# A three-branch decoder trunk in split fp32: convolution taps held from KI on, shorter steps for two pairs of stick heads, and one gate's turned copies tied to the newest weight parts

## The chip, the cores and the metric

The kernel runs on one core of one Trainium2 chip. The metric is the device time of one execution in microseconds; the time before is 2037.99 us, the median of 3 runs (2033.85 to 2039.13).

## What is computed

Two layers, each of which reads one normalised input of 256 tokens by 2048 channels, projects it with one matrix of 18064 columns, and feeds three token mixers, whose gated results are projected, merged and added to the input. Two of the mixers matter here:

```python
def stick_breaking_attention(q, k, v):          # branch C, 8 heads of 128
    z = einsum('bthd,bshd->bhts', q, k) * dh ** -0.5
    log_beta = log_sigmoid(z)
    log_keep = where(strict, log_sigmoid(-z), 0.0)
    after = cumsum(log_keep, axis=3, reverse=True) - log_keep
    a = where(strict, exp(log_beta + after), 0.0)
    return einsum('bhts,bshd->bthd', a, v)

y = lax.conv_general_dilated(y, conv_w, ...)     # branch B: causal depthwise convolution, 31 taps
y_c = (stick_breaking_attention(qc, kc, vc) * silu(zc)) @ w_c_out
```

Branch A scores keys with an indexer of 16 heads (its queries are QI below), keeps 64 keys for each query, and attends to those.

## The kernel before

**The weight stream.** Every matrix is read in units of 512 KB (128 partitions by 1024 elements; 544 elements in one stage). ScalarE (ACT) casts a unit to its high part `wh` (L265), VectorE (DVE) subtracts to get the low part `wl` (L270), and TensorE (PE) runs the unit's matmuls with both (all on L281). There are three buffers each for `wh` and `wl`, so the cast of a unit waits for PE to be done with the unit three before it.

**Background work.** Everything else is written as generators that are advanced from `background()` after a unit's matmuls: a `yield n` lets n units pass. `turns` come first, then the first two entries of `stages`; `finish()` runs all stages to their end at once. A scheduler then orders each engine's instructions ahead of time, so each engine works through a fixed list, and an instruction that waits holds up all behind it on its engine.

**Stick heads.** `stick(h0)` does two heads: scores on PE (L725, L728), then on ACT absolute value, table load, exponential and logarithm (L731 to L735), on DVE two combinations and the mask (L736 to L741), a split in parts `ph` and `pl` (L394, L395); after a pace of 10 units the prefix sums on PE (L747 to L752), then L753 on DVE, the exponential L754 on ACT, the mask L756 on DVE; after 5 more units the product with the values (L761, L763) and its copy L765 on ACT. The text numbers the pairs of heads 1 to 4. Pairs 1 and 2 run first, 3 and 4 after them.

**The stages around them**, in the order of PE: QA (queries of branch A, turned by a DMA transpose), KI (two units), VA with WI (eight units of 544 elements), KA (four units), then `finish()`, then QI (32 units in eight chunks), then the indexer beside the units of the merge gates, then branch A's attention, the gate of branch C (ZC) and of B (ZB).

**Taps.** Each of the 31 taps of the convolution, for each half of the channels, is four scalings on ACT (L439) and one addition on DVE (L442). They wait in a list; `low()`, which makes `wl`, releases one tap for each unit unless `hold[0]` is set. The last three of all are 228, 227 and 226 columns wide (4x228 and so on in the order).

**Turned copies.** `turn_in` sends a block through a DMA transpose and copies it back as 16-bit halves: one half on DVE (L187), the other on ACT (L189). With `bound` the copies may not stand ahead of the newest `wl` (DVE) and `wh` (ACT); without it the scheduler is free. `gate()` follows the copies with the SiLU (L417), the product (L418) and the split (L394, L395).

Of the kernel before, what the change touches and what calls it, by code (L numbers as in the profile page):

```python
# [34 lines left out]
TURN = (8, 8)  # L35
EARLY = (4, 6)
LATE = (6, 6)
MERGED = ((3, 7), (3, 6), (3, 5))
FAST = ((0, 0), (0, 1))
SCALE = float(128 ** -0.5)  # L40
# [5 lines left out]
O_QC, O_KC, O_VC, O_ZC, O_G = 7824, 8848, 9872, 10896, 11920  # L46
# [8 lines left out]
def trunk(ctx: ExitStack, tc: tile.TileContext, x, xt, w_in, w_a, w_b, w_c, w_out,  # L55
# [38 lines left out]
    def nm(s):  # L94
        uid[0] += 1
        return f"{s}_{uid[0]}"
# [29 lines left out]
    def acc_tile():  # L126
        return ap.tile([P, 2, 512], F32, tag="acc", name=nm("acc"))

    def t4(dt=F32):
        return tp.tile([P, 1024], dt, tag="t4", bufs=8, name=nm("t4"))  # L130
# [36 lines left out]
    def turn_in(src, dst, then=None, slots=True, turn=TURN, early=False):  # L167
        own, cols = words(slots)
        rows = own.rearrange("p (t w d) -> p t w d", t=NT, w=2)
        s16 = src.bitcast(U16).rearrange("p t (d w) -> p t d w", w=2)  # L170
        with tc.high_priority():
            for i in range(2):
                nc.scalar.copy(rows[:, :, i, :], s16[:, :, :, i])

        def steps():
            yield turn[0]
            with tc.high_priority() if turn in MERGED else nullcontext():
                for t in range(NT):
                    nc.sync.dma_start(cols.rearrange("p (g t) -> p g t", g=8)[:, :, t * P:(t + 1) * P],
                                      own[:, t * 1024:(t + 1) * 1024], transpose=True)  # L180
            yield turn[1]
            halves_ = cols.rearrange("p (w f t) -> p w f t", w=2, f=4)
            into = own.bitcast(F32).rearrange("p (f t) -> p f t", f=4) if dst is None else dst
            d16 = into.bitcast(U16).rearrange("p f (t w) -> p f t w", w=2)
            bound = turn == LATE or turn in MERGED
            with tc.issue_after(lows[0].ins) if bound else nullcontext(), tc.high_priority() if bound else nullcontext():
                nc.vector.tensor_copy(d16[:, :, :, 1], halves_[:, 1])  # L187
            with tc.issue_after(highs[0].ins) if bound else nullcontext(), tc.high_priority() if bound else nullcontext():
                (nc.vector.tensor_copy if early else nc.scalar.copy)(d16[:, :, :, 0], halves_[:, 0])  # L189
            if dst is None:  # L190
                then(into, cols.bitcast(F32).rearrange("p (f t) -> p f t", f=4))
            elif then is not None:
                then()

        turns.append([steps(), count[0] + 0])
        advance(turns[-1])

    def start(gen):
        stages.append([gen, 0])

    def finish():
        while stages:
            advance(stages[0])

    hold = [False]
# [145 lines left out]
    def chunk_W(w, c0, act):  # L351
        acc = acc_tile()
        for k0 in range(0, KD, 2):
            background(token_products([acc[:, t, :] for t in range(NT)], 512, unit(w, k0, 2, [(c0, 512)]), act, k0, 2, KD,
                                      range(NT)))
        return acc
# [58 lines left out]
    def gate(c0, o, b, w, hx, park=None, slots=True, turn=TURN):  # L415
        def gated(k, z, v):
            nc.scalar.activation(v, z, AF.Silu)  # L417
            nc.vector.tensor_mul(z, v, o[:, k:k + 4, :])  # L418
            b.extend(parts(4))
            split_at(b, k, 4, z)  # L420
            if park is not None:
                for i in range(k, k + 4, 2):
                    nc.gpsimd.dma_start(park[:, i:i + 2], part(b, slice(0, 2), i, 2))

        for k in range(0, KC, 4):
            turn_in(chunk_W(w, c0 + k * P, hx), None, partial(gated, k), slots, turn)
# [45 lines left out]
    parked = [dp.tile([P, KC, 2, S], F32R, name=f"parked{b}") for b in range(3)]  # L472
# [14 lines left out]
    for layer in range(DEPTH):  # L487
        w = w_in[layer]
        nw = cst[:, C_NW + layer * KD:C_NW + (layer + 1) * KD]
        pr = cst[:, C_PR + layer * P_END:C_PR + (layer + 1) * P_END]  # L490
        hx = parts(KD)
# [212 lines left out]
        qcT = slot()  # L704
# [3 lines left out]
        kcT, vc = slot(), slot()  # L708
        for h in range(0, NH, 4):
            turn_in(chunk_W(w, O_KC + h * P, hx), kcT[:, h:h + 4, :], early=True)  # L710
        vcr = vc.rearrange("p a b -> p (a b)").rearrange("p (t f) -> p t f", t=NT)
# [7 lines left out]
            return (b[:, :512].rearrange("p (h t) -> p h t", h=2)[:, :, 0:P],  # L719
                    b[:, 512:768].rearrange("p (h t) -> p h t", h=2))  # L720

        def stick(h0, qcT=qcT, kcT=kcT, vcr=vcr, diag=diag):
            ps = mm_tile()
            for q in range(2):
                nc.tensor.matmul(ps[:, q * S:(q + 1) * S], kcT[:, h0 + q, 0:P], qcT[:, h0 + q, :],  # L725
                                 start=True, stop=True)
            for q in range(2):
                nc.tensor.matmul(ps[:, 512 + q * P:512 + (q + 1) * P], kcT[:, h0 + q, P:S],  # L728
                                 qcT[:, h0 + q, P:S], start=True, stop=True)
            nk, lb = t4(), t4()  # L730
            ab = nc.scalar.activation(nk[:, :768], ps[:, :768], AF.Abs)  # L731
            with tc.issue_after(ab.ins):
                nc.scalar.preload_act_table_set("natural_log_exp_and_others")
            nc.scalar.activation(nk[:, :768], nk[:, :768], AF.Exp, scale=-1.0)
            nc.scalar.activation(nk[:, :768], nk[:, :768], AF.Ln, bias=1.0)  # L735
            nc.vector.scalar_tensor_tensor(lb[:, :768], ps[:, :768], 0.0, nk[:, :768],  # L736
                                           op0=ALU.min, op1=ALU.subtract)
            nc.vector.scalar_tensor_tensor(nk[:, :768], ps[:, :768], 0.0, nk[:, :768],
                                           op0=ALU.max, op1=ALU.add)
            for d in diag(nk):  # L740
                nc.vector.tensor_mul(d, d, smask2)  # L741
            pr_ = pair(768)
            split(*pr_, nk[:, :768])
            yield 10
            pc = mm_tile()
            for i, v in enumerate(pr_):
                nc.tensor.matmul(pc[:, :512], upper_r, v[:, :512], start=i == 0, stop=False)  # L747
            for i, v in enumerate(pr_):
                nc.tensor.matmul(pc[:, :512].rearrange("p (h t) -> p h t", h=2)[:, :, P:S], ones_r,
                                 v[:, 512:768].rearrange("p (h t) -> p h t", h=2), start=False, stop=i == 1)  # L750
            for i, v in enumerate(pr_):
                nc.tensor.matmul(pc[:, 512:768], upper_r, v[:, 512:768], start=i == 0, stop=i == 1)  # L752
            nc.vector.tensor_sub(lb[:, :768], lb[:, :768], pc[:, :768])  # L753
            nc.scalar.activation(lb[:, :768], lb[:, :768], AF.Exp)  # L754
            for d in diag(lb):
                nc.vector.tensor_mul(d, d, smask2)  # L756
            yield 5
            po = mm_tile()
            for q in range(2):
                vs_ = slice((h0 + q) * P, (h0 + q + 1) * P)  # L760
                nc.tensor.matmul(po[:, q * S:(q + 1) * S], vcr[:, 0, vs_], lb[:, q * S:(q + 1) * S],  # L761
                                 start=True, stop=False)
                nc.tensor.matmul(po[:, q * S + P:(q + 1) * S], vcr[:, 1, vs_],  # L763
                                 lb[:, 512 + q * P:512 + (q + 1) * P], start=False, stop=True)
            nc.scalar.copy(qcT[:, h0:h0 + 2, :], po[:, :512].rearrange("p (h t) -> p h t", h=2))  # L765

        settle()
        for h0 in range(0, NH, 2):
            start(stick(h0))

        qaT = slot()
        def spin(q4):
# [8 lines left out]

        for h in range(0, NH, 4):
            turn_in(chunk_W(w, O_QA + h * P, hx), qaT[:, h:h + 4, :], partial(spin, qaT[:, h:h + 4, :]))
        kaT = t4()[:, :2 * S].rearrange("p (c t) -> p c t", c=2)
        ki = tp.tile([P, 2 * S], F32R, tag="ki", bufs=1, name=nm("ki")).rearrange("p (i c t) -> p i c t", i=2, c=1)
        rope(chunk_T(w, O_KI, P, hx, KD), None, partial(split, ki[:, 0], ki[:, 1]))
# [11 lines left out]
        nc.scalar.copy(wp_[64:128], wf[64:128, :, 1])  # L798
        rope(chunk_T(w, O_KA, 256, hx, KD), kaT)

        hold[0] = True
        finish()
        qa2 = slot(F32R).rearrange("p a b -> p (a b)").rearrange("p (i h t) -> p i h t", i=2, h=NIH)
        qb2 = [slot(F32R).rearrange("p a b -> p (a b)").rearrange("p (h t) -> p h t", h=NIH) for _ in range(2)]
# [194 lines left out]

        for j in range(2, 4):  # L1000
            early(1, j)
        gate(O_ZC, qcT, [], w, hx, parked[2])
        gb = []
        gate(O_ZB, cv, gb, w, hx, slots=False, turn=LATE)
        finish()
# [21 lines left out]
        start(mixtures())  # L1027
        gate(O_ZA, qaT, [], w, hx, parked[0], slots=False, turn=LATE)
        finish()
# [28 lines left out]
        def combine(gate_of=None):  # L1058
            gx = gb
            for n, b in enumerate((1, 2, 0)):  # L1060
# [4 lines left out]
                for j in range(4):  # L1065
# [20 lines left out]
                    if n == 2 and j < 3:  # L1086
                        mx[j], = parts(4)
                        turn_in(mg[j // 2][:, j % 2], None, partial(turned, j), False, MERGED[j])
                    elif n == 2:
# [118 lines left out]
        def emit_x(xc, accs, q, c0, ts):  # L1208
# [10 lines left out]
            else:  # L1219
                x_squares([xc[:, t, :] for t in ts], ssq, q, ts)  # L1220
                if q < 3:
                    turn_in(xc, None, lambda z, v: x_parts(z, xn, c0 // P, nwn, 4), False, MERGED[2])

# [88 lines left out]
```

## Time and profile before

| | |
|---|---|
| median of 3 runs | 2037.99 us (2033.85 to 2039.13) |
| the profiled execution | 2035.96 us, span 2034.1 us |
| PE busy | 2008.7 us, 99% of the span |
| VectorE, ScalarE, GpSimd busy | 1562.2 us (77%), 1401.9 us (69%), 97.1 us (5%) |
| HBM | 213 GB/s over the span |
| mean granted clock of TensorE | 0.997 |

Times of views are microseconds from the start of the span. A row of the timeline gives start, duration, engine, line, operation, out<-in, shapes and how many; in square brackets stands how long the engine had been idle and what ended that. Rows that follow each other on ACT and DVE overlap by about 0.1 us in print, so that a run of them takes about 0.1 us less for each than the printed durations. The two layers run the same program of work; in the stages here, rows of layer 1 stand about 1008 us behind those of layer 0.

### The profile page before, as it was taken

The page shows a single profiled execution, that of the slowest core. Times are in us where ns is not written, and L with a number is a line of the kernel's source. Part 1 is how long each engine was busy: PE and PEld are TensorE (multiplying, and loading weights), DVE is VectorE, ACT ScalarE, POOL GpSimd, SP SyncE. Part 2 cuts the span into 40 slices and gives each one's busy share as a digit, 9 for nine tenths or more (in the row PEclk, how much of TensorE's full clock was granted, in tenths as well). Part 3 has the DMA queues.
Part 4 walks back from the last instruction along what each step waited for, and adds up shares of the span by engine and source line. Part 5 has one row for each costly group of instructions (what it writes and reads, how often), then busy time and mean ns, then how long its engine had stood idle before and what let it go on. Part 6 is the DMA issues. An engine that isn't in the chain of part 4 may idle for free. (4 is left out here: it accounts for less than half of the span.)

```text
span 2034.1 us, 26740 instructions
## 1 busy us (share of the span) xinstructions
PE 2008.7 (99%) x9566; PEld 1700.3 (84%) x9566; DVE 1562.2 (77%) x1708; ACT 1401.9 (69%) x1968; POOL 97.1 (5%) x156
## 2 busy tenths in 40 slices
PE   9999998999999999999999999999999999999998
PEld 7888888988788888888888888889888888888887
DVE  8688888787578888866676888878866788788665
ACT  7899796648766555556658987965588665556653
POOL 0000000000001100110000000000000012002100
PEclk9999999999999999999999999999999999999999
DMA  8787675766888877889967776656678898778983
GB/s 279 216 226 214 181 167 173 222 195 191 234 244 264 269 247 232 263 270 264 258 201 211 218 216 187 168 176 206 189 206 235 241 266 285 224 240 264 270 283 126
DMA packets 340278, 458.60 MB, mean 225 GB/s; under 512 B 109104, under 2 KB 159024, under 8 KB 340016
## 3 DMA queue, kind: packets, MB, share of 16 engines
q1 hardware_dynamic: 327040, 420.82, 70.9%
q0 software_dynamic: 11648, 33.56, 5.0%
q10 hardware_dynamic: 1456, 2.51, 0.4%
q8 instruction: 75, 1.23, 0.2%
q14 instruction: 59, 0.48, 0.1%
HBM read 413.30 MB, written 20.97 MB: 213 GB/s over the span
## 5 line engine op out<-in xcount | busy, mean ns | idle before, releaser
L281 PE MATMUL acc<-wh,s 128*128 128x512 f32 (+2 forms) x4736 | 1155.4, 386 | 2.2 <-ACT wh L265 2.0
L270 DVE TENSOR_TENSOR wl<-raw,wh 128x1024 fp32r<-128x1024 f32 (+1 forms) x714 | 858.2, 1208 | 319.2 <-ACT wh L265 313.5
L281 PEld LDWEIGHTS acc<-wh,s 128*128 128x128 f32 x4736 | 875.7, 188 | 179.6 <-ACT wh L265 3.9
L265 ACT CAST wh<-raw 128x1024 fp32r<-128x1024 f32 (+1 forms) x713 | 738.7, 1039 | 390.0 <-PE acc L281 317.9
L281 PE MATMUL acc<-wl,s 128*128 128x512 f32 (+2 forms) x2368 | 622.7, 385 | 0.8 <-DVE wl L270 0.8
L281 PEld LDWEIGHTS acc<-wl,s 128*128 128x128 f32 x2368 | 439.5, 188 | 90.3 <-DVE wl L270 1.3
L439 ACT ACTIVATE t<-s,cst 128x255 f32<-128x255 f32 (+14 forms) x480 | 199.0, 487 | 0.0
L442 DVE TENSOR_TENSOR s<-s,t 128x1020 f32<-128x1020 f32 (+14 forms) x120 | 138.6, 1155 | 1.5 <-ACT t L439 1.1
L281 PE MATMUL acc<-s,wh 128*128 128x384 f32 (+1 forms) x608 | 125.6, 348 | 0.0
L281 PE MATMUL mm<-wh,s 128*128 128x512 f32 x448 | 119.7, 389 | 0.0
L281 PEld LDWEIGHTS acc<-s,wh 128*128 128x128 f32 x608 | 104.2, 189 | 3.1
L281 PEld LDWEIGHTS mm<-wh,s 128*128 128x128 f32 x448 | 84.1, 188 | 17.4
L265 ACT CAST wh<-s 128x1024 fp32r<-128x1024 f32 x32 | 33.6, 1050 | 68.4 <-DVE s L1106 53.3
L281 PEld LDWEIGHTS acc<-s,wl 128*128 128x128 f32 x608 | 79.6, 191 | 0.9
L281 PE MATMUL acc<-s,wl 128*128 128x192 f32 (+1 forms) x608 | 80.1, 273 | 0.0
L232 POOL COPY sm<-sm 128x3 f32<-128x3 f32 x64 | 47.1, 735 | 564.6 <-ACT sm L231 564.6
L281 PE MATMUL mm<-wl,s 128*128 128x512 f32 x224 | 69.1, 390 | 0.0
L265 ACT CAST wh<-t 128x1024 fp32r<-128x1024 f32 x32 | 33.6, 1050 | 37.7 <-DVE t L1106 27.4
L270 DVE TENSOR_TENSOR wl<-s,wh 128x1024 fp32r<-128x1024 f32 x32 | 39.2, 1225 | 26.3 <-ACT wh L265 26.1
L902 POOL DMA_DIRECT2D gates<-t x8 | 6.0, 744 | 1115.5 <-ACT t L901 1066.3
L281 PEld LDWEIGHTS mm<-wl,s 128*128 128x128 f32 x224 | 41.9, 188 | 9.0 <-DVE wl L270 0.4
L270 DVE TENSOR_TENSOR wl<-t,wh 128x1024 fp32r<-128x1024 f32 x32 | 39.1, 1222 | 9.9 <-ACT wh L265 7.1
(241 smaller groups left out, 1286.3 us busy)
## 6 DMA issues: line engine op xcount, KB each, us to landing
raw<-in_w_in_dram SPq DMA_DIRECT2D x570, 512.0 KB, 4.3
raw<-in_w_out_dram SPq DMA_DIRECT2D x64, 512.0 KB, 5.1
raw<-in_w_b_dram SPq DMA_DIRECT2D x32, 512.0 KB, 5.3
raw<-in_w_c_dram SPq DMA_DIRECT2D x32, 512.0 KB, 5.1
raw<-in_w_a_dram SPq DMA_DIRECT2D x32, 512.0 KB, 5.6
parked<-s POOLq DMA_DIRECT2D x16, 512.0 KB, 5.5
t<-gates POOLq DMA_DIRECT2D x16, 512.0 KB, 6.6
s<-parked POOLq DMA_DIRECT2D x32, 256.0 KB, 5.7
```

The source lines that it names most:

```text
L232: seen = nc.gpsimd.tensor_copy(copy[:, :3], mark)
L265: highs[0] = nc.scalar.copy(u[1], u[0])
L270: sub = nc.vector.tensor_sub(u[2], u[0], u[1].bitcast(F32))
L281: newest[0] = nc.tensor.matmul(o, lhsT, rhs, start=start, stop=stop, skip_group_check=True)
L439: nc.scalar.activation(o[:, i, :S - d], yT[:, c, :S - d], AF.Copy, scale=wq)
L442: nc.vector.tensor_add(to, to, o[:, :, :S - d])
L902: nc.gpsimd.dma_start(gates[b][:, :, j * 512:(j + 1) * 512].rearrange("t p d -> p t d"), sg_)
```

## The change

Three edits.

1. `hold[0] = True` moves from ahead of `finish()` to ahead of KI, so no tap is released during KI, VA and KA either. The last three taps of each layer are released after QI.
2. The pace of pairs 3 and 4 becomes 7 and 4 units; pairs 1 and 2 keep 10 and 5.
3. ZC's gate gets a pair of steps of its own, (8, 9) for (8, 8), and its copies are `bound`.

```diff
+OWN = (8, 9)
+STICK = ((10, 5), (7, 4))
...
-            bound = turn == LATE or turn in MERGED
+            bound = turn in (LATE, OWN) or turn in MERGED
...
-        def stick(h0, qcT=qcT, kcT=kcT, vcr=vcr, diag=diag):
+        def stick(h0, pace, qcT=qcT, kcT=kcT, vcr=vcr, diag=diag):
...
-            yield 10
+            yield pace[0]
...
-            yield 5
+            yield pace[1]
...
-            start(stick(h0))
+            start(stick(h0, STICK[h0 // 4]))
...
             turn_in(chunk_W(w, O_QA + h * P, hx), qaT[:, h:h + 4, :], partial(spin, qaT[:, h:h + 4, :]))
+        hold[0] = True
         kaT = t4()[:, :2 * S].rearrange("p (c t) -> p c t", c=2)
...
         rope(chunk_T(w, O_KA, 256, hx, KD), kaT)
-        hold[0] = True
         finish()
...
-        gate(O_ZC, qcT, [], w, hx, parked[2])
+        gate(O_ZC, qcT, [], w, hx, parked[2], turn=OWN)
```

The order of the SP and POOL queues is the same before and after; PE's differs only where the stick heads stand. In rows of the changed kernel, line numbers are 2 higher than in the profile (3 higher from KI to the end of KA). Names: `s_80` is the convolution's input, `s_336` the queries of QA, `s_137` the queries and then the output of the stick heads, `t_439` and `t_436` pair 3's weights, `t_447` and `t_444` pair 4's.

**ACT, from the taps in KI on.** Before:

```order
L439 ACTIVATE t_409_2417<-s_80_536,cst 128x230 x2
L439 ACTIVATE t_413_2441<-s_80_536,cst 128x229 x4
L439 ACTIVATE t_421_2473<-s_80_536,cst 128x228 x4
L265 CAST wh_2632<-raw_2631 128x544
L765 COPY s_137_854<-mm_2495 128x512
L306 COPY ev_2535<-acc_2466 128x256
L439 ACTIVATE t_426_2507<-s_80_536,cst 128x227 x3
L406 COPY ev_2538<-ev_2535 64x256
```

The same place after:

```order
L441 ACTIVATE t_409_2417<-s_80_536,cst 128x230 x2
L441 ACTIVATE t_413_2441<-s_80_536,cst 128x229 x4
L767 COPY s_137_854<-mm_2489 128x512
L191 COPY s_336_2021<-s_379_2247 128x1024
L267 CAST wh_2614<-raw_2613 128x544
L191 COPY s_336_2021<-s_414_2461 128x1024
L308 COPY ev_2523<-acc_2466 128x256
L767 COPY s_137_854<-mm_2517 128x512
L408 COPY ev_2526<-ev_2523 64x256
```

The taps of 228 columns and less are gone from here, and the two turned copies of QA, which stood among VA's and KA's casts, have moved in.

**DVE, where the last stick heads end**, between KA and QI. Before:

```order
L411 TENSOR_TENSOR t_415_2464<-t_415_2464,ev_2884 128x512
L780 TENSOR_TENSOR s_336_2021<-s_336_2021,ev_2715 128x512
L753 TENSOR_TENSOR t_439_2580<-t_439_2580,mm_2837 128x768
L753 TENSOR_TENSOR t_447_2618<-t_447_2618,mm_2870 128x768
L270 TENSOR_TENSOR wl_3014<-raw_3012,wh_3013 128x1024
L756 TENSOR_TENSOR t_439_2580<-t_439_2580,cst 128x2x128
L756 TENSOR_TENSOR t_439_2580<-t_439_2580,cst 128x256
L756 TENSOR_TENSOR t_447_2618<-t_447_2618,cst 128x2x128
```

After (pair 3's L755 stands 15 rows further up):

```order
L397 TENSOR_TENSOR pl_2610<-t_443_2599,ph_2609 128x768
L782 TENSOR_TENSOR s_336_2021<-s_336_2021,ev_2697 128x512
L758 TENSOR_TENSOR t_436_2562<-t_436_2562,cst 128x2x128
L758 TENSOR_TENSOR t_436_2562<-t_436_2562,cst 128x256
L272 TENSOR_TENSOR wl_2935<-raw_2933,wh_2934 128x1024
L309 TENSOR_TENSOR ev_2869<-acc_2763,ev_2869 128x512
L755 TENSOR_TENSOR t_444_2600<-t_444_2600,mm_2786 128x768
L411 TENSOR_TENSOR t_415_2464<-ev_2869,cst 128x512
L412 TENSOR_TENSOR ev_2872<-ev_2872,cst 128x512
L413 TENSOR_TENSOR t_415_2464<-t_415_2464,ev_2872 128x512
L758 TENSOR_TENSOR t_444_2600<-t_444_2600,cst 128x2x128
```

Pairs 3 and 4 no longer end together: pair 3's mask stands ahead of the rotation of KA (L309 to L413), pair 4's behind it.

On ACT the same place reads, after:

```order
L267 CAST wh_2934<-raw_2933 128x1024
L308 COPY ev_2869<-acc_2763 128x512
L767 COPY s_137_854<-mm_2863 128x512
L408 COPY ev_2872<-ev_2869 64x512
L409 COPY ev_2872<-ev_2869 64x512
L267 CAST wh_2970<-raw_2969 128x1024
L756 ACTIVATE t_444_2600<-t_444_2600 128x768
```

Pair 3's output copy (L767) stands ahead of pair 4's exponential (L756); before, both exponentials stood ahead of both output copies. On PE pair 3's product with the values now stands ahead of QI's first unit and pair 4's behind that unit; before, both stood inside QI's third unit.

**ACT, at ZC's gate.** Before:

```order
L394 CAST ph_4989<-t_814_4801 128x1024
L189 COPY s_835_4927<-s_835_4927 128x1024
L265 CAST wh_5030<-raw_5029 128x1024
L417 ACT_TABLE_LOAD
L417 ACTIVATE s_835_4927<-s_835_4927 128x1024
```

After:

```order
L267 CAST wh_5263<-raw_5262 128x1024
L191 COPY s_835_4927<-s_835_4927 128x1024
L267 CAST wh_5290<-raw_5289 128x1024
L419 ACTIVATE s_835_4927<-s_835_4927 128x1024
L267 CAST wh_5314<-raw_5313 128x1024
```

The second half's copy `s_835` now stands behind 12 more units' casts.

## The prediction

> **What bounds the kernel now.** I read the page's busy times first, then PE's waits, then the clock in stretches around the longest wait, then the timeline of that place, engine by engine.
>
> ```profile
> span 2034.1 us, 26740 instructions
> PE 2008.7 (99%) x9566; PEld 1700.3 (84%) x9566; DVE 1562.2 (77%) x1708; ACT 1401.9 (69%) x1968; POOL 97.1 (5%) x156
> ```
>
> PE bounds the whole: it is idle for 25.4 us of 2034.1. Only that idle time, and time in which PE is busy but slow, can be won. PE's waits:
>
> ```profile
> PE mm L761 <- DVE t L756: 9.1, 2, 4.6
> PE acc L281 <- ACT wh L265: 2.0, 3, 1.1
> PE mm L725 <- ACT s L765: 0.8, 2, 0.4
> ```
>
> More than a third of the idle time is one wait in each layer: stick pairs 3 and 4 end in `finish()`, and their product L761 waits 4.6 us for the mask L756. The stretches show what follows (their columns: length; busy PE, PEld, DVE, ACT, POOL; granted clock; DMA share; GB/s):
>
> ```profile
> 320.00:325.00 5.00, 1.13 (x3) 0.98 (x4) 5.00 (x9) 3.81 (x5) 0.00 (x0) 0.86 0.44 112
> 1333.00:1337.00 4.00, 4.00 (x15) 3.46 (x15) 3.24 (x6) 0.58 (x1) 0.00 (x0) 0.50 0.33 111
> 550.00:560.00 10.00, 8.86 (x39) 7.01 (x39) 4.37 (x5) 4.67 (x5) 1.11 (x2) 1.00 1.02 274
> ```
>
> After 4.6 us of idleness the clock is down to 0.50, and PE, though "busy", does half the work. After the idle 1.1 us at ZC (550 to 560) it stays at 1.00. PE's timeline there, with the first row of layer 1's same stretch and its end:
>
> ```profile
> 277.36 0.60 PE L761 MATMUL mm<-t,s 128*128 128x256 f32 x2
> 278.59 2.07 PE L281 MATMUL acc<-s,wh 128*128 128x512 f32 x8
> 282.69 1.24 PE L281 MATMUL acc<-wh,s 128*128 128x272 f32 x8
> ...
> 298.27 1.99 PE L281 MATMUL acc<-s,wh 128*128 128x512 f32 x8
> ...
> 306.63 0.40 PE L747 MATMUL mm<-ph,upper_r 128*128 128x512 f32 x1
> 307.57 2.00 PE L281 MATMUL acc<-s,wh 128*128 128x512 f32 x8
> 312.94 1.57 PE L281 MATMUL acc<-s,wh 128*128 128x384 f32 x8
> 315.22 1.59 PE L281 MATMUL acc<-s,wh 128*128 128x384 f32 x8
> 323.87 1.19 PE L761 MATMUL mm<-t,s 128*128 128x256 f32 x2 [4.57 <-DVE t L756]
> 328.76 1.57 PE L281 MATMUL acc<-s,wh 128*128 128x384 f32 x8
> 1290.45 1.24 PE L281 MATMUL acc<-wh,s 128*128 128x272 f32 x8
> 1337.80 1.58 PE L281 MATMUL acc<-s,wh 128*128 128x384 f32 x8
> ```
>
> From VA's first unit (282.69) to QI's fourth (328.76) PE takes 46.07 us, in layer 1 47.35. The differences of starts give undisturbed lengths: a pair's product 1.23 (277.36 to 278.59), a KA unit 2.79 (298.27 to 306.63 are three), prefix sums 0.94, a QI unit 2.28.
>
> **The shorter steps (edit 2), with the taps out of the way (edit 1).** I follow the new order of ACT and DVE with durations of these rows:
>
> ```profile
> 277.19 3.88 ACT L439 ACTIVATE t<-s,cst 128x230 f32<-128x230 f32 x10
> 285.21 0.40 ACT L406 COPY ev<-ev 64x256 f32<-64x256 f32 x1 [1.73 <-DVE ev L307]
> 290.64 1.28 ACT L733 ACT_TABLE_LOAD   x1
> 291.93 0.65 ACT L265 CAST wh<-raw 128x544 fp32r<-128x544 f32 x1
> ```
>
> ```profile
> L265 ACT CAST wh<-raw 128x1024 fp32r<-128x1024 f32 x11 | 11.4, 1045 | 2.3 <-PE acc L281 2.2
> L189 ACT COPY s<-s 128x1024 uint16<-128x1024 uint16 x2 | 2.7, 1341 | 0.0
> L776 ACT COPY ev<-s 64x512 f32<-64x512 f32 x4 | 2.5, 620 | 0.6 <-DVE t L411 0.5
> L765 ACT COPY s<-mm 128x512 f32<-128x512 f32 x4 | 2.3, 578 | 3.7 <-PE mm L763 3.7
> L394 ACT CAST ph<-t 128x768 fp32r<-128x768 f32 x2 | 1.7, 832 | 0.0
> L270 DVE TENSOR_TENSOR wl<-raw,wh 128x1024 fp32r<-128x1024 f32 x11 | 13.4, 1222 | 2.7 <-ACT wh L265 2.0 <-PE acc L281 0.5
> L778 DVE TENSOR_TENSOR s<-s,cst 128x512 f32<-128x512 f32 x4 | 2.8, 689 | 0.0
> L395 DVE TENSOR_TENSOR pl<-t,ph 128x768 fp32r<-128x768 f32 x2 | 1.9, 954 | 0.1
> L756 DVE TENSOR_TENSOR t<-t,cst 128x256 f32<-128x256 f32 x4 | 1.4, 422 | 0.0
> 282.47 0.76 DVE L187 COPY s<-s 128x1024 uint16<-128x1024 uint16 x1 [1.76 <-DMA s<-s]
> ```
>
> In a run of them each takes about 0.1 us less than printed.
>
> *Pair 3's prefix sums* now stand ahead of KA, not behind its third unit. ACT from 277.19: six tap scalings (2.3) to 279.5; pair 1's output copy, QA's first turned copy and a cast to 281.8; the second turned copy waits for its transpose, which lands at 282.47 (DVE's row), to 283.7; four small copies of KI and pair 2, with the hand-over to DVE that cost 1.73 us of idleness before, to 285.4. Then five casts of 0.54 (2.7), three copies like L776 (1.9), four operations of 768 columns (3.0), two table loads (2.6), KI's part (0.3), KA's first cast (0.95): 296.9; `ph` is there at 297.7. DVE has KA's first `wl` ahead of `pl`: 298.1, then `pl` to 299.0. PE has VA done at about 297.4 (298.27 less the 0.4 us wait of L725, which goes since pair 2's copy L765 now comes before KI's rotation, and half a microsecond of slow restart, an estimate). So PE waits some 1.5 us in two pieces and starts KA at 299.8.
>
> *Pair 4's prefix sums* stand inside KA's fourth unit. PE: 4 x 2.79 + 0.94 from 299.8 is 311.9. DVE is back to back from 299.0: five `wl` (5.7), four operations of 768 columns (3.5), three of 512 (1.8), two parts of VA (0.7), two masks (1.3): 312.0. So pair 3's product meets its mask within 0.1 us and ends at 313.2.
>
> *Pair 4's product* stands one QI unit later, at 315.5. What it needs starts only at 313.2, since ACT is a fixed list: pair 3's output copy (0.5), KA's two rotations (1.3), a cast (0.95), the exponential (0.84), then DVE's mask (0.75), hand-overs 0.1: 317.7. PE waits 2.2 us. This term is the firmest, since all of it hangs on one event. The product, QI's second and third units (1.23 + 4.56) and 0.2 for the restart bring the fourth to 323.7: 5.1 us earlier than 328.76. Layer 1 loses 1.3 more now (47.35 against 46.07) by a longer slow stretch: 6.4. Together **11.5 us**.
>
> The sum assumes that 2.2 us of idleness leave the clock alone. Bounds: nothing, as after 1.1 us, or the whole price after 4.6 us. In layer 0 that price is 1.7 us (323.87 to 328.76 is 4.89; two products, 2.46, and the rest of the QI unit that they interrupt, about 0.7, are 3.2), in layer 1 1.3 more. I take nothing: 2.2 is nearer 1.1. The Trainium skill ("TensorE: Matmul & The Clock Gate", Part 1) says that the clock halves after a whole idle window of about 3.4 us, in windows that run freely; the halving to 0.50 agrees, and by the rule 2.2 us is safe, so the sum stays.
>
> The table loads speak against the shortened path: two of them lie ahead of `ph`. The cast at 291.93 starts 0.01 us behind the load's end, so I charge 1.29. The Trainium skill ("ScalarE: Activation LUTs", What ACT_TABLE_LOAD costs) adds about 1.38 us of draining to each load, 2.66 in all. That is rival D.
>
> **The held taps (edit 1)** leave 1.6 us of ACT for each of three taps and 1.1 us of DVE beside the indexer.
>
> ```profile
> 290.21 1.09 DVE L442 TENSOR_TENSOR s<-s,t 128x904 f32<-128x904 f32 x1
> 431.40 1.21 DVE L270 TENSOR_TENSOR wl<-raw,wh 128x1024 fp32r<-128x1024 f32 x1
> 435.62 1.07 PE L281 MATMUL acc<-wl,s 128*128 128x512 f32 x4
> ```
>
> DVE then runs up to 3.3 us late. The tightest `wl` that I found there ends at 432.61, and PE uses it at 435.62 (the one before it at 432.90), 3.0 us later: hidden, or 0.3 us uncovered in each layer. I charge 0.3 for both; with no cover it would be 6.6.
>
> **ZC's gate (edit 3).** ACT stands still for a transpose, and the casts behind it with it:
>
> ```profile
> 556.04 1.37 ACT L189 COPY s<-s 128x1024 uint16<-128x1024 uint16 x1 [5.30 <-DMA s<-s]
> 575.52 1.05 ACT L265 CAST wh<-raw 128x1024 fp32r<-128x1024 f32 x1 [1.67 <-PE acc L281]
> PE acc L281 <- ACT wh L265: 0.6, 1, 0.6
> ```
>
> Behind 12 more casts the copy finds its data landed. What PE loses to this are its waits for `wh`, 2.0 us in all, less the one in the first 30 us (0.6, the last row); I take **1.4** (bounds 0 and 2.0). The gate's work of 3.3 us moves beside B's gate, where ACT idles 1.67 us in each unit (575.52).
>
> **Sum.** 11.5 + 1.4 - 0.3 = 12.6 us off 2035.96, the profiled execution's own time: 2023.4. The median of the three runs is 2.0 higher, so theirs would be 2025.4; I say 2024.5, between the two, and add the same 1.1 to each rival's sum.
>
> **Rivals.**
>
> A. *All stick waits vanish.* ACT and DVE rows were padded by waits in my walk; were they quicker by 2 us, nothing would wait. Against it: pair 4's chain of 4.5 us behind one QI unit of 2.28. PE's path from VA to QI's fourth unit would be 14.7 for VA (15.58 less the 0.9), 11.2, 1.9, 2.5 and 6.8, in all 37.0: 9.1 and 10.4 less than now, which with the rest is 2016.5.
>
> B. *Pair 4's wait passes the point where the clock halves.* For it: a late `wl` or cast adds to the 2.2. With 3.5 us of waiting in both layers, and prices of 1.7 and 3.0, the gain falls by 7.3 to 5.3: 2032.
>
> C. *Slower:* the wait moves to pair 3's prefix sums ahead of KA. ScalarE's list has no idle place left there. Turned copies now stand ahead of eight casts, so a transpose that lands late holds VA's casts as well. If the second lands 4 us later than 282.47, pair 3's parts come 4 us later, PE idles over 5, and the clock halves: 8 and 4.7 us in both layers are the whole gain. From there on the kernel is slower, 2042 at 289. Against it: SP's order is the same, and the landing is in the trace.
>
> D. *Each table load costs 1.4 us more.* Pair 3 would come 2.8 later in each layer: 2030. The row of 291.93 speaks against it.
>
> **Chances.** Forecast 0.70, A 0.12, B 0.12, C 0.04, D 0.02. 0.3% (6.1 us) is about what a measurement of this kernel can tell from no change. Faster: the forecast but for 0.03, A, D and a little of B, 0.82; within 0.3%: 0.14; slower: 0.04. The range takes in most of A and of B: 2016 to 2032.
>
> **What would show it.** Right: L761's two waits fall from 4.6 to about 2.2 each, a new one of 1 to 1.5 us for `pl` at L747 stands ahead of KA, granted clock 1.00 from VA to QI, the L725 wait gone, no ACT wait for a DMA at ZC, PE idle about 19 us in all. Wrong: a clock under 0.9 near QI (B), no wait at L761 (A), long waits of ACT on `s` in VA (C), or waits for `wl` beside the indexer.

## The result, and the profile after

The changed kernel takes 2025.95 us (median of four runs, 2025.41 to 2026.60), the kernel before 2036.53 in the same comparison: a ratio of 0.9948, with a 95% interval of 0.9931 to 0.9966. It is faster by 10.6 us. The forecast was 2024.5 with a range of 2016 to 2032. The total came out; which of the edits earned it did not, as the experiments show. Of the eleven executions of e1 below, one ran in a slower state (4080.92 us) and counts in no ratio.

The profiled execution took 2025.73 us. The head of its page, and PE's waits (waiter and what it waited for; us in total, times, longest):

```profile
span 2024.0 us, 26716 instructions
PE 2006.2 (99%) x9566; PEld 1698.9 (84%) x9566; DVE 1560.7 (77%) x1708; ACT 1399.7 (69%) x1966; POOL 98.5 (5%) x156
```

```profile
PE mm L763 <- DVE t L758: 4.1, 2, 2.1
PE mm L749 <- DVE pl L397: 1.8, 2, 0.9
PE acc L283 <- ACT wh L267: 1.5, 4, 0.7
```

PE is idle for 17.8 us instead of 25.4. The wait for the masks has fallen from 4.6 to 2.0 us in each layer, and a new one of 0.9 for `pl` stands ahead of KA. The scores' wait for pair 2's copy is gone, and so are two of 0.6 and 0.5 us in each layer for `ph` and `pl` of pair 4's prefix sums. (All names at the matmul, copy and mask lines are two lines further down than before: L761 is L763, L756 is L758.) PE's timeline from the end of VA to QI, in layer 0, and from the product on in layer 1 (rows in between are left out):

```profile
296.26 1.28 PE L283 MATMUL acc<-wh,s 128*128 128x272 f32 x8 [0.18 <-ACT wh L267]
299.34 0.51 PE L749 MATMUL mm<-pl,upper_r 128*128 128x512 f32 x1 [0.90 <-DVE pl L397]
312.36 0.59 PE L763 MATMUL mm<-t,s 128*128 128x256 f32 x2
313.59 1.66 PE L283 MATMUL acc<-s,wh 128*128 128x384 f32 x8
318.15 0.67 PE L763 MATMUL mm<-t,s 128*128 128x256 f32 x2 [2.03 <-DVE t L758]
320.09 2.61 PE L283 MATMUL acc<-s,wh 128*128 128x384 f32 x8
323.41 1.59 PE L283 MATMUL acc<-s,wh 128*128 128x384 f32 x8
325.70 1.59 PE L283 MATMUL acc<-s,wh 128*128 128x384 f32 x8
1321.29 0.67 PE L763 MATMUL mm<-t,s 128*128 128x256 f32 x2 [2.05 <-DVE t L758]
1322.86 2.91 PE L283 MATMUL acc<-s,wh 128*128 128x384 f32 x8
1326.52 1.57 PE L283 MATMUL acc<-s,wh 128*128 128x384 f32 x8
```

Behind the wait of 2.03 us the first half of QI's second unit takes 2.61 us instead of 1.59, and in layer 1 2.91. The same stretches in numbers, with ZC's (columns as before: length; busy PE, PEld, DVE, ACT, POOL; granted clock; DMA share; GB/s):

```profile
318.00:325.00 7.00, 6.85 (x34) 6.65 (x35) 6.36 (x10) 3.68 (x6) 0.00 (x0) 0.76 0.26 77
1320.00:1326.00 6.00, 4.71 (x20) 4.58 (x21) 5.63 (x10) 3.93 (x7) 0.00 (x0) 0.72 0.32 94
550.00:560.00 10.00, 10.00 (x46) 8.24 (x45) 4.34 (x4) 6.19 (x6) 0.00 (x0) 1.00 0.74 232
```

So the clock still falls in QI. Finer windows put it at 0.50 for 3.41 us in each layer (318.80 to 322.21 and 1322.32 to 1325.73); before, it was 3.41 us in layer 0 (from 323.62) and 6.82 us in layer 1 (from 1330.55). At ZC PE is now busy throughout (8.86 of 10 us before).

One measure serves all that follows: the stretch from the start of VA's first unit to the start of QI's fourth. It was 46.07 us in layer 0 and 47.35 in layer 1; it is now 43.05 (282.65 to 325.70) and 43.11. With nothing to wait for the forecast had put it at 37.0.

### The profile page after: what moved, and what is told of

Its sections match the earlier page's. It is cut to its first block, busy times and chain, and to the rows that moved or that the text cites. A ratio compares the mean times of both kernels' runs of the same rounds, so it can differ in the third digit from the quotient of the medians.

```text
span 2024.0 us, 26716 instructions
## 1 busy us (share of the span) xinstructions
PE 2006.2 (99%) x9566; PEld 1698.9 (84%) x9566; DVE 1560.7 (77%) x1708; ACT 1399.7 (69%) x1966; POOL 98.5 (5%) x156
## 3 DMA queue, kind: packets, MB, share of 16 engines
q8 instruction: 75, 1.23, 0.2%
## 5 line engine op out<-in xcount | busy, mean ns | idle before, releaser
L272 DVE TENSOR_TENSOR wl<-t,wh 128x1024 fp32r<-128x1024 f32 x32 | 39.1, 1222 | 10.2 <-ACT wh L267 7.5
```

The source lines that it names most:

```text
L272: sub = nc.vector.tensor_sub(u[2], u[0], u[1].bitcast(F32))
```

## The experiments

The kernels were timed in five comparisons. Each ratio is to the kernel before in the same comparison, whose median lay between 2034.89 and 2036.53 us, so times from different comparisons (the changed kernel; e1 to e4; e5 to e8; e9 to e11; e12) can be off against each other by 1.6 us, the spread of these medians. Stretches and waits are those of the one profiled execution.

| kernel | time, us | ratio to before, 95% | stretch, layers 0 and 1 | longest mask wait |
|---|---|---|---|---|
| before | 2036.53 | 1 | 46.07, 47.35 | 4.6 |
| changed kernel | 2025.95 | 0.9948 [0.9931, 0.9966] | 43.05, 43.11 | 2.1 |
| e1 steps alone | 2038.02 | 1.0006 [0.9997, 1.0015] | 47.10, 48.03 | 4.0 |
| e2 held taps alone | 2023.77 | 0.9938 [0.9925, 0.9952] | 41.09, 41.17 | 1.0 |
| e3 ZC alone | 2033.41 | 0.9988 [0.9980, 0.9997] | 47.26, 46.87 | 4.6 |
| e4 changed, pair 4's chain first | 2019.18 | 0.9917 [0.9902, 0.9932] | 39.10, 39.09 | none |
| e5 held taps and ZC | 2022.67 | 0.9936 [0.9923, 0.9949] | 41.22, 40.96 | 1.0 |
| e6 e4 with one table load fewer | 2025.17 | 0.9952 [0.9939, 0.9965] | 41.38, 42.80 | 0.8 |
| e7, e8 e4 with later masks (one run each) | 2023.01, 2023.59 | | 40.74, 40.43; 41.39, 40.82 | 1.0; 1.5 |
| e9 one tap held | 2033.82 | 0.9990 [0.9981, 0.9998] | 46.21, 46.49 | 5.2 |
| e10 e5, chains of pairs 3 and 4 first | 2020.24 | 0.9924 [0.9911, 0.9936] | 39.82, 39.81 | 0.6 |
| e11 e4 with steps 8 and 4 | 2019.86 | 0.9921 [0.9908, 0.9935] | 39.53, 38.84 | none |
| e12 before, chains of pairs 3 and 4 first | 2026.53 | 0.9959 [0.9945, 0.9972] | 41.34, 42.34 | 0.9 |

### Each edit by itself (e1, e2, e3, e5)

e1 keeps the shorter steps, puts `hold[0] = True` back ahead of `finish()`, and calls ZC's gate as before:

```diff
-        hold[0] = True
         kaT = t4()[:, :2 * S].rearrange("p (c t) -> p c t", c=2)
...
+        hold[0] = True
         finish()
...
-        gate(O_ZC, qcT, [], w, hx, parked[2], turn=OWN)
+        gate(O_ZC, qcT, [], w, hx, parked[2])
```

> The shorter steps alone (the taps stay where they were, the ZC gate as before). Theory (both are needed): three taps, 1.6 us of ACT each, stand in ACT's list between KI and KA, so the masks come up to 4.8 us later than in the changed kernel and PE waits for them again: at most 4 us faster than before, 2033 to 2037. Rival (the steps do it all): the 8 to 9 us of the two stick edits come without the taps' move: 2028.

Measured: 2038.0 us, no gain at all (the interval of the ratio spans 1). PE's waits in e1:

```profile
PE mm L763 <- DVE t L758: 8.0, 2, 4.0
PE mm L749 <- ACT ph L396: 4.9, 4, 1.6
```

In the kernel before, PE waited 2.2 us in all at the prefix sums (L747 there):

```profile
PE mm L747 <- ACT ph L394: 1.2, 2, 0.6
PE mm L747 <- DVE pl L395: 1.0, 2, 0.5
```

The wait for the masks is 4.0 us instead of 4.6, but that for the parts `ph` and `pl` has grown from 2.2 to 4.9 us, since the prefix sums are asked for earlier. The theory's direction holds; even its 4 us were too many.

e2 keeps the held taps alone; `STICK = ((10, 5), (10, 5))`, and ZC's gate as before.

> The held taps alone (the steps stay 10 and 5, the ZC gate as before). Theory (both are needed): pairs 3 and 4 still end together in QI and their masks, though ACT has 4.8 us less ahead of them, are asked for a QI unit or two earlier; the wait at the product L763 stays over 3 us in each layer: at most 4 us faster than before, 2033 to 2037. Rival (the taps were the whole delay): the wait falls under 1 us, the clock stays at 1.00, and the time falls by 8 or more: 2028.

Measured: 2023.8 us. The rival won: the held taps alone give 12.4 us (ratio 0.9938), no less than the whole change's 10.6 (the two intervals overlap). The theory, that both stick edits are needed, falls. PE's rows at the two products in layer 0, and the stretches around them:

```profile
315.01 0.67 PE L763 MATMUL mm<-t,s 128*128 128x256 f32 x2 [1.04 <-DVE t L758]
...
318.48 0.67 PE L763 MATMUL mm<-t,s 128*128 128x256 f32 x2 [0.94 <-DVE t L758]
```

```profile
312.00:318.00 6.00, 4.41 (x28) 3.74 (x26) 5.96 (x10) 4.96 (x7) 0.00 (x0) 1.00 0.55 168
318.00:325.00 7.00, 6.52 (x44) 6.45 (x45) 6.81 (x11) 4.65 (x7) 0.00 (x0) 1.00 0.27 77
```

The one wait of 4.6 us has become two of about 1 us, 3.5 us apart, and the clock stays at 1.00.

e3 keeps ZC's gate alone.

> The ZC gate's copies behind the newest parts alone. Theory: the stall in the first stretch after 550 us and the one near 1565 us vanish, worth 1.4 + 0.6 = 2.0 us by the distances between matmuls of the two traces: 2034.5, ratio 0.999. Rival (it only moved the loss to B's gate): no difference, 2036.5.

Measured: 2033.4 us, ratio 0.9988, thus 0.6 to 4.1 us off. The theory's 2.0 lies inside, the rival's nothing outside. PE is busy for 10.00 of 10 us at 550 and at 1560.

e5 is the changed kernel with steps of 10 and 5, that is without edit 2.

> The changed kernel without the shorter steps (held taps and ZC gate only, steps 10 and 5). Theory (the shorter steps cost time once the taps are held: they turn two waits of about 1 us, which leave the clock at 1.00, into one of 2.03 us, which does not, and put 0.9 us of waiting for pl ahead of KA): the 2023.8 of the held taps alone less ZC's 2.0 to 2.7: 2021.1 to 2021.8, 4 to 5 us faster than the changed kernel. Rival (edits add up otherwise, and ZC is worth nothing beside the held taps): 2023.8.

Measured: 2022.7 us, 3.3 below the changed kernel's 2025.95 (the two were not timed side by side: their runs, 2021.0 to 2023.3 and 2025.4 to 2026.6, do not overlap, but the intervals of their ratios do, and the ratios put the difference at 2.4). The stretches say it more firmly, 41.22 and 40.96 against 43.05 and 43.11: beside the held taps, the shorter steps cost 4.0 us in the two layers' stretches together, and 2.9 between the two profiled executions as a whole.

### Why the taps matter: time or order (e9, e12)

The taps' 4.8 us of ACT end long before the masks. The last of them in the kernel before:

```profile
289.44 0.48 ACT L439 ACTIVATE t<-s,cst 128x226 f32<-128x226 f32 x1
```

What differs later is DVE's list. In layer 0 of the kernel before it has both subtractions (L753; what they need, the prefix sums, is done at 307.6 and 312.9) behind all of KA's rotation and the first half of QA's:

```
L307 TENSOR_TENSOR ev_2881<-acc_2770,ev_2881 128x512
L780 TENSOR_TENSOR s_336_2021<-s_336_2021,ev_2709 128x512
L409 TENSOR_TENSOR t_415_2464<-ev_2881,cst 128x512
L778 TENSOR_TENSOR s_336_2021<-s_336_2021,cst 128x512
L779 TENSOR_TENSOR ev_2715<-ev_2715,cst 128x512
L410 TENSOR_TENSOR ev_2884<-ev_2884,cst 128x512
L270 TENSOR_TENSOR wl_2989<-raw_2987,wh_2988 128x1024
L411 TENSOR_TENSOR t_415_2464<-t_415_2464,ev_2884 128x512
L780 TENSOR_TENSOR s_336_2021<-s_336_2021,ev_2715 128x512
L753 TENSOR_TENSOR t_439_2580<-t_439_2580,mm_2837 128x768
L753 TENSOR_TENSOR t_447_2618<-t_447_2618,mm_2870 128x768
```

With the taps held (e2), the planner (the scheduler that orders each engine's list) writes pair 3's subtraction (there L755) ahead of KA's sum (L309) and pair 4's ahead of most of the rotations. The rows of the two traces, before and then e2:

```profile
320.44 1.81 DVE L753 TENSOR_TENSOR t<-t,mm 128x768 f32<-128x768 f32 x2
```

```profile
311.85 0.95 DVE L755 TENSOR_TENSOR t<-t,mm 128x768 f32<-128x768 f32 x1
...
315.72 0.95 DVE L755 TENSOR_TENSOR t<-t,mm 128x768 f32<-128x768 f32 x1
```

Before, the subtraction starts without any idle time of DVE ahead of it: it is not waiting for data, it is queued. It comes 8.6 us earlier with the taps held.

e9 holds the taps from the end of KI, so that one of the three is held.

> The kernel before, with the taps held from the end of KI instead of ahead of it: two of the three taps still run in front of the stick pairs, one is held. Theory (each tap delays ACT's list by its 1.6 us, and the masks with it): the wait at L763 falls by about 1.6 us in each layer, from 4.6 to 3.0, still long enough to lower the clock: 2036 less 3.2, 2033. Rival (the wait depends on the taps as a whole, for instance on ACT's last idle place): as with all three held, 2024, or as with none, 2036.

Measured: 2033.8 us, where the theory had 2033; the interval of 0.4 to 3.9 us off includes it and leaves out both ends of the rival. But the reason given was wrong. The wait did not shrink (5.2 us). DVE's subtraction starts at 317.24, and 3.2 us earlier is not enough: PE asks for the product one QI unit earlier as well.

e12 leaves the taps in, and changes the order alone:

```diff
+            with tc.high_priority(offset=URGENT) if h0 >= NH // 2 else nullcontext():
-            nc.vector.tensor_sub(lb[:, :768], lb[:, :768], pc[:, :768])
+                nc.vector.tensor_sub(lb[:, :768], lb[:, :768], pc[:, :768])
...
```

(the exponential and the masks stand under the same line).

> The kernel before (taps not held, steps 10 and 5, ZC gate as before) with one thing changed: the subtraction, exponential and masks of pairs 3 and 4 are put first. In the kernel before, DVE's list has both subtractions behind KA's and QA's rotations, though the prefix sums are done 8 us earlier. Theory (the held taps helped by the order that the planner then writes, not by the 4.8 us of ACT that they free): with the order put right and the taps left in, PE waits under 1 us at each product, clock 1.00: the 4.6 us of waiting and 1.7 to 3.0 us of slow clock in each layer go, less 1: 2022 to 2025. Rival (the taps' own time is what delays the masks): waits of 3 us or more stay, 2031 or above.

Measured: 2026.5 us, ratio 0.9959. The masks' wait is 0.9 us, in one layer only. Between the theory's 2025 and the rival's 2031 it is near the theory: the order is most of it, about two thirds of e2's 12.4 us. The profiled execution's stretches, 41.34 and 42.34, are 4.7 and 5.0 shorter than before; but that execution, 2022.6 us, was the fastest of the five, and where the others (2026.3 to 2028.1) lost their 4 to 5 us no trace shows. What is left of the taps' own time stands elsewhere, ahead of pair 4's prefix sums, where PE now waits 1.8 us in each layer instead of the 1.1 before (layer 0, then layer 1):

```profile
310.75 0.50 PE L749 MATMUL mm<-ph,upper_r 128*128 128x512 f32 x1 [0.61 <-ACT ph L396]
312.44 0.50 PE L749 MATMUL mm<-pl,upper_r 128*128 128x512 f32 x1 [1.20 <-DVE pl L397]
1312.57 0.50 PE L749 MATMUL mm<-ph,upper_r 128*128 128x512 f32 x1 [0.62 <-ACT ph L396]
1314.27 0.50 PE L749 MATMUL mm<-pl,upper_r 128*128 128x512 f32 x1 [1.19 <-DVE pl L397]
```

Windows of 3.41 us, two in layer 0 and two in layer 1 (the last section says why they are cut so):

```profile
308.61:312.02 3.41, 2.03 (x12) 1.43 (x10) 2.92 (x4) 3.35 (x8) 0.00 (x0) 1.00 0.68 178
312.03:315.44 3.41, 3.00 (x18) 2.85 (x19) 2.95 (x5) 2.70 (x5) 0.00 (x0) 1.00 0.38 129
1312.13:1315.54 3.41, 1.77 (x8) 1.38 (x9) 2.95 (x7) 3.41 (x5) 0.00 (x0) 1.00 0.66 190
1315.54:1318.95 3.41, 3.41 (x13) 3.17 (x13) 3.23 (x5) 1.76 (x4) 0.00 (x0) 0.50 0.27 67
```

The same two waits lower the clock in layer 1 and not in layer 0.

e10 is e5 with the same priority: held taps and right order.

> Held taps and ZC gate, steps 10 and 5, and the subtraction, exponential and masks of pairs 3 and 4 put first. Theory (the two waits of 1.04 and 0.94 at L763 in each layer come from the rotation's work ahead of the exponentials): both fall under 0.4, and there is no wait for pl ahead of KA: 2022.7 less 2.6 to 4: 2018.7 to 2020.1. Rival (they come from the prefix sums, which end later with the long steps): 2022 to 2023.

Measured: 2020.2 us, just beyond the upper edge of the theory. One of the two waits at the product is gone, the other is 0.6. No wait stands ahead of KA, as expected, but a new one of 0.9 us for `pl` stands at pair 4's prefix sums (L749). Against e12 the stretches are 1.5 and 2.5 shorter: what the taps' time itself costs there once the order is right (layer 1's part includes the slow clock).

### The remaining wait and the clock (e4, e7, e8)

e4 is the changed kernel with the line of e12 for pair 4 only (`h0 == NH - 2`).

> The changed kernel with pair 4's subtraction, exponential and masks put ahead of other work on ACT and DVE: its chain then hangs on its own prefix sums, not on pair 3's output copy and KA's rotation. PE gets pair 4's product in the middle of QI's first unit. Theory (the wait and the slow clock after it both come from that fixed order): PE waits under 0.4 us there, granted clock 1.00 through the stretch, and each layer is 2.0 us (wait) + 1.3 to 1.7 us (slow clock) shorter: 2018.9 to 2019.8. Rival (only the wait goes, the clock falls for another reason): 2022. Rival (the work put behind it, KA's rotation and the turned copies, stalls PE instead): 2025 to 2026.

Measured: 2019.2 us, ratio 0.9917, as the theory said. PE does not wait at either product, and the stretch keeps its clock:

```profile
315.45 0.59 PE L764 MATMUL mm<-t,s 128*128 128x256 f32 x2
```

```profile
318.00:325.00 7.00, 7.00 (x50) 7.00 (x50) 6.47 (x10) 6.24 (x9) 0.00 (x0) 1.00 0.26 77
```

It has the lowest median of all, with e11 and e10 so close that the intervals do not part them, and stands 6.8 us below the changed kernel (another comparison; 6.5 between the profiled executions). Its stretches are 4.0 shorter in each layer: 2.0 of wait, 1.7 of slow clock, and 0.3 left over, about what VA's last cast had cost. Some 1.5 us of the two layers' 8.0 came back outside the stretch.

e7 and e8 lengthen e4's wait: the masks are multiplied in three and four times more, with `for d in diag(lb) * 4` and `* 5` for pair 4.

> The kernel with pair 4's chain put first, and its masks multiplied in three more times (the same zeros and ones, so the same values): 3 x 0.72 us of DVE ahead of pair 4's product, to set the length of PE's wait. PE should wait 1.3 to 1.5 us there. Theory (the clock falls when most of a 3.4 us stretch is idle): clock stays at 1.00. Rival (anything beyond 1.1 us lowers it): clock under 0.9 behind the wait.

> The same with four more times, 4 x 0.72 us. PE should wait 1.8 to 2.1 us. Theory: the clock falls to about 0.75 in the 7 us behind it, as behind the 2.03 us of the changed kernel, if the idle time falls into one stretch of 3.4 us; in one of the two layers it may not. Rival (the wait of 2.03 us was not what lowered it): clock 1.00 in both layers.

Measured: PE waits 1.01 and 1.03 us in e7, 1.49 in both layers of e8, less than expected in both, because the planner moved the product back among QI's matmuls. e8's row, and the stretch behind it:

```profile
318.65 0.67 PE L764 MATMUL mm<-t,s 128*128 128x256 f32 x2 [1.49 <-DVE t L759]
```

```profile
318.00:325.00 7.00, 6.35 (x43) 6.28 (x44) 5.19 (x9) 4.66 (x7) 0.00 (x0) 1.00 0.35 105
```

The clock stays at 1.00. So "anything beyond 1.1 us lowers it" falls. e8 missed its length, but e1 has a longer single wait, 1.62 us for `ph` in each layer, and its clock stays at 1.00 there too (last section).

### Two that did not pay (e6, e11)

e6 leaves out the table load of the second pair (`if h0 % 4 == 0:` around the preload) in e4.

> The kernel with pair 4's chain put first (2019.2), and the table load left out in the second pair of each two, for which the table is already loaded. Theory (the second load, 1.28 us, stands right ahead of VA's last cast and of pair 3's ph, and makes PE wait for them): the waits at VA's last unit (up to 0.9) and for pl at L749 (0.9 in each layer) fall to about 0.2 together; 1 us less in each layer: 2017.0 to 2017.6. If a load also drained ACT for 1.4 us on top of its own row, up to 1.4 us more room, but PE has nothing left to gain there. Rival (DVE, not ACT, is what pl waits for): 2019.2, waits as before.

Measured: 2025.2 us, slower than e4 by 6.0 (another comparison; 4.7 between the profiled executions); both theories missed. The freed 1.28 us was given to other work: the planner put a copy, an exponential and KA's first cast ahead of `ph`, whose cast then starts 15.5 us after VA's start (at 282.69) instead of 14.3 (at 283.11 in e4). ACT's row in e4, then in e6:

```profile
297.45 0.83 ACT L396 CAST ph<-t 128x768 fp32r<-128x768 f32 x1
```

```profile
298.19 0.82 ACT L396 CAST ph<-t 128x768 fp32r<-128x768 f32 x1
```

PE waits 0.64 for `ph`, 1.12 for `pl` and 0.75 at the product in each layer, and in layer 1 the clock falls behind the first two:

```profile
1300.34 0.51 PE L750 MATMUL mm<-ph,upper_r 128*128 128x512 f32 x1 [0.64 <-ACT ph L396]
1301.96 0.50 PE L750 MATMUL mm<-pl,upper_r 128*128 128x512 f32 x1 [1.12 <-DVE pl L397]
```

```profile
1304.00:1306.00 2.00, 2.00 (x6) 1.52 (x6) 2.00 (x4) 0.00 (x0) 0.00 (x0) 0.50 0.98 282
```

The run tells of the order, not of what a load costs.

e11 is e4 with `STICK = ((10, 5), (8, 4))`.

> The changed kernel with pair 4's chain put first, and steps of 8 and 4 for the last two pairs: pair 3's prefix sums come behind KA's first unit, when pl is there. Theory: the wait of 0.9 for pl goes in each layer, and about half of it comes back at pair 3's masks, since DVE is back to back there: 2019.2 less 0.5 to 1.8: 2017.4 to 2018.7. Rival (DVE sets the end either way): 2019.2.

Measured: 2019.9 us, no difference from e4: the rival. The wait ahead of KA went, and 0.6 us of waiting for `pl` came back at pair 4's prefix sums.

## Why the prediction was right in total and wrong in its parts

- *The shorter steps, with the taps out of the way: 11.5 us.* This term failed. The two edits were costed as one, with the gain under the steps, and the taps charged as a loss of 0.3. Apart, the held taps give 11.2 us of stretch (46.07 to 41.09, 47.35 to 41.17), the steps alone lose 1.7, and the steps beside the held taps lose 4.0. The walk followed the new order's chains; it never asked which edit had made that order. The row that would have shown it was in the trace of before: L753 at 320.44, 13 us after pair 3's prefix sums and 8 after pair 4's, with no idle time of DVE ahead of it.
- *The clock: "I take nothing: 2.2 is nearer 1.1."* Failed: the cost came to the other bound, 1.7 us. The wait was 2.03 us, and the clock fell. In layer 0 the product took 1.94 instead of 1.23 (318.15 to 320.09) and QI's second unit 3.32 instead of 2.28, 1.75 in all; in layer 1 1.57 and 3.66, 1.72. Of the 11.5 predicted 7.3 were measured (3.02 and 4.24); these 3.5 us are most of the difference. Rival B asked for 3.5 us of waiting before it set in: its mechanism came true at 2.03, and with it a sign that the prediction had named for being wrong, a clock under 0.9 near QI. By the last section's limit, a single wait of this length lowers the clock at about two of three positions (an estimate: 1.64 of its 2.03 us have to fall into one piece of 3.41), so in a layer the wrong guess had about one chance in three of passing unseen.
- *The walk itself held.* KA's start was put at 299.8 and the first KA unit is at 300.14; pair 3's product meets its mask without a wait; pair 4's product was put at 317.7 after 2.2 us of waiting and stands at 318.15 after 2.03. One wait was missed, VA's last cast (0.18, and 0.27 in layer 1), which stands behind the second table load. VA ended at 297.95, not 297.4: the half microsecond of slow restart that was taken out of it was not there. KA's start hung on `pl`, so this only shortened the wait ahead of it, to 0.9 from the 1.5 of the walk.
- *The table loads: 1.29 us each, no drain.* Held:

```profile
294.27 1.28 ACT L735 ACT_TABLE_LOAD   x1
295.56 1.59 ACT L267 CAST wh<-raw 128x544 fp32r<-128x544 f32 x2
```

  The cast starts 0.01 us behind the load's end. The Trainium skill ("ScalarE: Activation LUTs", What ACT_TABLE_LOAD costs) has the load's duration right at about 1283 ns; its drain beside the load does not show in these rows.
- *ZC's gate: 1.4 us (0 to 2.0).* Mechanism right, size a little low: the distances between matmuls give 1.4 in layer 0 and 0.6 in layer 1, and e3 2.7 by the medians (0.6 to 4.1). ACT waits for no transpose there any more.
- *The held taps beside the indexer: 0.3 us.* Covered: PE is busy for all 45 us from 400 to 445 in the changed kernel.
- *Rivals A, C, D.* None came. A's 2016.5 needs all waits gone; e4 took those at the products away and came to 2019.2.

By the profiled executions the change is worth 10.2 us (2035.96 to 2025.73), against 12.6 in the sum: the two stick edits together gave 4.2 less than forecast, everything outside the stretch 1.9 more than the 1.1 charged. That the total came within 1.5 us of 2024.5 is in part luck: the two errors have opposite signs.

## What to carry to other kernels

When a change has several edits, cost each against the kernel before by itself; a chain that is walked in the final order tells the end time, not which edit bought it. Where an engine waits for a result, look whether its producer was waiting or merely queued: DVE's subtractions stood 8 and 13 us behind their data with DVE busy, and a priority on the subtraction, the exponential and the masks gave the kernel before 8.4 us by itself (e12), about two thirds of what the held taps gave; on top of the changed kernel it took away the wait and the slow clock (e4). Freed time on an engine with a planned order goes to whatever the planner puts there (e6), so read the new list before counting it.

## What the runs showed of the hardware

How much idleness lowers PE's clock was not where it had been put. A single wait of 0.90, 1.04, 1.49 or 1.62 us left it at 1.00 each time; one of 2.03 and 2.05 us lowered it in both layers (0.76 and 0.72 over the 6 to 7 us behind); 4.0 us and more always did. Two waits of 0.6 and 1.2 us with one matmul between them, 1.8 us in all within 2.3, lowered it in one layer of two in e6 and in one of two in e12, with the same rows. So a whole idle stretch of 3.4 us isn't needed.

The traces show what decides. The clock falls and returns on a grid: inside the program it is at 0.50 for 3.41 us or twice that, and in one trace these places lie a whole number of 3.413 us apart (the changed kernel's two, at 318.80 and 1322.31, 294 such pieces). Cut along the grid, layer 0 of the changed kernel and then of e1 (whose wait of 1.62 us ends at 302.24) read as follows, e12 as above:

```profile
315.38:318.79 3.41, 1.38 (x11) 1.18 (x11) 3.03 (x6) 3.35 (x5) 0.00 (x0) 1.00 0.44 145
318.80:322.21 3.41, 3.41 (x14) 3.23 (x13) 3.41 (x6) 1.84 (x4) 0.00 (x0) 0.50 0.41 116
300.55:303.96 3.41, 1.79 (x11) 1.52 (x11) 3.28 (x4) 3.41 (x5) 0.00 (x0) 1.00 0.92 247
303.97:307.38 3.41, 3.41 (x22) 3.07 (x22) 3.41 (x5) 3.31 (x6) 0.00 (x0) 1.00 1.01 323
```

PE is idle for 2.03 us of the changed kernel's first piece, and the clock is down in the next; for 1.62 us of e1's, and it stays. In e12 the two waits leave 1.64 us idle in one piece of layer 1, and the clock falls; in layer 0 the edge at 312.02 cuts the second wait, 1.38 us lie in one piece, and it stays. All 14 traces part in this way: the clock falls 12 times inside the program, each time behind a piece with 1.64 us of idleness or more, and behind no piece with 1.63 or less. The limit in these traces is thus about half a piece, and near it the place of the wait in the grid decides, which the program does not set. The ends of matmuls are modelled, so the last digit is not firm, and no run was made to test the limit. A fall costs about 1.7 us, half of 3.41, where PE has work throughout (1.75 and 1.72 in the changed kernel).

The Trainium skill ("TensorE: Matmul & The Clock Gate", Part 1) has the clock halve after a whole idle window of about 3.4 us, in windows that run freely. The pieces of 3.41 us agree with it; the waits of 2.03 us, inside one piece that was not wholly idle, disagree, and the measurement decides.
